# The input projection of a gated attention and convolution layer, split into a first phase of seven-product groups without attention and a second phase that holds all attention

## The chip, the cores and the metric

The kernel runs on one core of a Trainium2 chip. The metric is the device time of one execution in microseconds (us). Three runs of the kernel before took 3035.85, 3040.83 and 3042.26 us, so the median is 3040.83 us. In the text, TensorE is PE (PEld its weight loads), VectorE is DVE, ScalarE is ACT, GpSimd is POOL and SyncE, which here only issues DMAs, is SP.

## What is computed

One layer on 2048 positions of 1024 channels, all in float32. An input norm, one wide projection into nine pieces of 1024 columns, an attention branch and a convolution branch side by side, a gated merge, an output projection and a norm:

```python
h = _layer_norm(x, ln_in_g, ln_in_b)
q, k, v, z_sb, c_val, c_gate, z_cv, g_sb, g_cv = split(h @ w_in)       # 1024 -> 9 * 1024
o_sb = stick_breaking_attention(q, k, v)                               # 16 heads of 64
y_sb = (o_sb * silu(z_sb)) @ w_sb_proj
u = causal_depthwise_conv(c_val * sigmoid(c_gate), conv_w, conv_b)     # 31 taps
u = silu(_layer_norm(u, conv_ln_g, conv_ln_b))
y_cv = (u * silu(z_cv)) @ w_cv_proj
merged = sigmoid(g_sb) * y_sb + sigmoid(g_cv) * y_cv
out = _layer_norm(ALPHA * h + merged @ w_out, ln_post_g, ln_post_b)
```

The attention weight of a key is the sigmoid of its logit times the product of one minus the sigmoid over all keys between it and the query, so each row of the score matrix needs a running product along the keys.

## The kernel before

**Arithmetic.** Every float32 matrix is split exactly into two float32r parts, `a = hi + lo` (`split`, lines 112 to 114: ACT rounds into `hi` with L113, DVE subtracts into `lo` with L114). A product of two such matrices is three passes: hi times hi, hi times lo and lo times hi. A block of the projection is 128 columns of a weight by a chunk of 512 positions: 8 contraction blocks by 3 passes, 24 PE instructions of 128x512 (L194), in four "pieces" of six.

**Stages.** Positions are reversed in time and kept as four chunks of 512, in two halves: half 1 (chunks 3 and 2) is done first, then half 0 (chunks 1 and 0). The input norm writes the transposed activations of a half into `xh` and `xl`. `Fill` is the stream of projection pieces: for each half all 72 blocks of `w_in` (`fill_qkv` for k, q, v; `z`; `u`, which is c_val and c_gate; `c`, `g` and `h` for the other gates), then the two branch projections, and at the end the output projection. Weights are loaded and split again for each half (`load_w`, L148 issues the load, lines 113 and 114 split).

**Attention.** For each of 8 pairs of heads and each half of the queries: the logits of 128 queries (two PE passes, L572 and L573), ACT's sigmoid into `nb` (L575), a scan on DVE that makes the running product (L578, up to 1024 keys each), PE transposes of it (`tp`, L601), a split of the transposed tile (`th` on ACT, `tl` on DVE, L113 and L114), and the product with v (`pv`, L617). A "turn" is one transposed tile of 512 columns with its split and its product. Queries of half 0 read all keys, those of half 1 half of them, so about three quarters of the attention belong to half 0.

**What sets the order.** PE runs in the order in which the program is written. Two streams are woven by hand: the list of attention items and the `Fill` pieces, by a proportion (`spans`). Attention of half 1 lies beside the projection of half 1, as soon as a pair's q, k and v are there; attention of half 0 lies beside the projection of half 0 and the two branch projections of half 1. The other engines follow a scheduler's order, in which some evacuations are raised by `tc.high_priority`. The convolution is 31 taps on DVE (L402, one instruction of 128x512 for a tap on half the positions), issued one step at a time beside projection pieces, `PACE` = 0.83 steps for each piece (`slow_step`). All plain DMAs are issued by SP in one order (`dma`, L94; `load_w`, L148).

The two lines on which a product's cost rests:

```python
for n, (l, r) in enumerate(((wh, xh), (wh, xl), (wl, xh))):
    nc.tensor.matmul(box["ps"], lhsT=l[:, kb], rhs=r[kb], start=(kb == 0 and n == 0), stop=(kb == KB - 1 and n == 2))
```

## Time and profile before

| | |
|---|---|
| median of three runs | 3040.83 us |
| span of the profiled execution | 3036.5 us |
| DMA, mean over the span | 150 GB/s |
| ACT, share of the span | 42% |
| POOL, share of the span | 3% |

The profiled execution's span is 4.3 us below the median of the runs. The profile shows one execution. Its rows of groups read: line, engine, operation, output tile `<-` inputs, shape and count, then busy time in us and mean duration of one in ns, then the idle time of the engine before them with what ended it. Durations of consecutive instructions of one engine overlap, so the spacing of starts, not the duration, is an instruction's cost when its engine is never idle. Rows of windows give, for a stretch from A to B us, each engine's busy time with the number of instructions, the granted clock of PE as a share, the DMA engines' busy share and the rate of DMA in GB/s. The granted clock is 0.996 in the mean over the span.

### The profile page before, as it was taken

What the parts mean: (1) busy time and instruction counts of PE and PEld (TensorE: products, weight loads), DVE (VectorE), ACT (ScalarE), POOL (GpSimd) and SP (SyncE); (2) the same over time, 40 slices, a digit from 0 to 9 for tenths busy, and PEclk for the clock granted to TensorE, in tenths of its full rate; (3) what the DMA queues carried; (4) which work ended last, traced back from release to release, by engine and by line L of the source; (5) the groups of instructions that cost most, each with busy time, mean ns of one, the idle gap of its engine ahead of it and who ended that gap; (6) DMA issues with size and microseconds to landing.
All of it is one profiled execution on the core that took longest, in us unless ns stands there. A gap on an engine that the chain in (4) does not pass through costs nothing.

```text
span 3036.5 us, 41850 instructions
## 1 busy us (share of the span) xinstructions
PE 2959.8 (97%) x15304; PEld 2484.1 (82%) x15304; DVE 2381.6 (78%) x3175; ACT 1269.5 (42%) x2308; POOL 88.3 (3%) x178
## 2 busy tenths in 40 slices
PE   7999999999999999999999999999999999999998
PEld 6888888888887788888888888887888878878886
DVE  5587787777879888788879888879887788856656
ACT  5333333333336344444445444445445455533222
POOL 1000000000000000000000000000000000000000
PEclk9999999999999999999999999999999999999999
DMA  7543443434434533343335344335545666685552
GB/s 269 172 144 112 148 139 117 149 125 130 139 101 140 169 100 110 114 131 123 111 112 189 103 143 141 99 103 175 164 155 161 191 224 191 208 280 197 161 189 78
DMA packets 260221, 455.92 MB, mean 150 GB/s; under 512 B 30384, under 2 KB 55088, under 8 KB 259888
## 3 DMA queue, kind: packets, MB, share of 16 engines
q1 hardware_dynamic: 260016, 453.25, 46.0%
q8 instruction: 120, 1.97, 0.3%
q14 instruction: 85, 0.70, 0.1%
HBM read 292.70 MB, written 160.43 MB: 149 GB/s over the span
## 4 chain that ended last, share of the span: by engine, by line
PE 73%; DVE 11%; issue 10%; DMA 3%; ACT 2%; POOL 1%; SPq 0%; DVEq 0%; POOLq 0%; ACTq 0%
PE mm L194 52%; PE pv L617 7%; PE tp L601 6%; DVE nb L578 3%; PE lg L573 3%; PE lg L572 3%; DVE tl L114 2%; DVE wlo L114 1%; DVE cy L402 1%; PE mo L900 1%; DMA st<-ydq 1%; DMA ydq<-st 1%; DVE xl L114 1%; DVE st L494 0%; DVE st L493 0%
## 5 line engine op out<-in xcount | busy, mean ns | idle before, releaser
L194 PE MATMUL mm<-xh,whi 128*128 128x512 f32 x2816 | 1144.5, 406 | 1.7 <-ACT whi L113 1.5
L194 PE MATMUL mm<-xh,wlo 128*128 128x512 f32 x2816 | 1110.1, 394 | 1.4 <-DVE wlo L114 1.4
L194 PE MATMUL mm<-xl,whi 128*128 128x512 f32 x2816 | 1106.2, 393 | 1.2 <-DVE xl L114 1.2
L194 PEld LDWEIGHTS mm<-xh,wlo 128*128 128x128 f32 x2816 | 530.0, 188 | 120.9 <-DVE wlo L114 1.9
L194 PEld LDWEIGHTS mm<-xl,whi 128*128 128x128 f32 x2816 | 532.9, 189 | 86.8 <-DVE xl L114 2.4
L194 PEld LDWEIGHTS mm<-xh,whi 128*128 128x128 f32 x2816 | 531.5, 189 | 86.4 <-ACT whi L113 1.9
L113 ACT ACTIVATE th<-tp 128x512 fp32r<-128x512 f32 (+1 forms) x576 | 329.4, 572 | 613.9 <-PE tp L601 606.1
L114 DVE TENSOR_TENSOR tl<-tp,th 128x512 fp32r<-128x512 f32 (+1 forms) x576 | 376.5, 654 | 180.1 <-ACT th L113 178.2
L575 ACT ACTIVATE nb<-lg 128x512 f32<-128x512 f32 (+3 forms) x640 | 334.9, 532 | 308.9 <-PE lg L573 299.0
L578 DVE TENSOR_TENSOR_SCAN nb<-nb,dd 128x256 f32<-128x256 f32 (+7 forms) x256 | 345.1, 1350 | 42.2 <-ACT nb L575 41.5
L601 PE MATMUL tp<-ident,nb 128*128 128x128 f32 x2176 | 337.8, 274 | 20.3 <-DVE nb L578 18.2
L578 DVE TENSOR_TENSOR_SCAN nb<-nb,zero 128x1024 f32<-128x1024 f32 x128 | 300.0, 2346 | 36.5 <-ACT nb L575 36.2
L601 PEld LDWEIGHTS tp<-ident,nb 128*128 128x128 f32 x2176 | 263.4, 140 | 77.9 <-DVE nb L578 22.5
L113 ACT ACTIVATE whi<-wraw 128x512 fp32r<-128x512 f32 x352 | 217.6, 629 | 261.1 <-PE mm L194 238.8
L617 PE MATMUL pv<-tl,v 128*128 128x256 f32 (+1 forms) x1152 | 292.1, 282 | 12.2 <-DVE tl L114 11.6
L114 DVE TENSOR_TENSOR wlo<-wraw,whi 128x512 fp32r<-128x512 f32 x352 | 237.4, 682 | 80.0 <-ACT whi L113 52.9
L617 PE MATMUL pv<-th,v 128*128 128x256 f32 (+1 forms) x1152 | 299.5, 281 | 0.0
L572 PE MATMUL lg<-k,qd 128*128 128x512 f32 (+3 forms) x640 | 246.4, 386 | 11.6 <-ACT nb L575 7.0
L617 PEld LDWEIGHTS pv<-tl,v 128*128 128x128 f32 x1152 | 218.1, 189 | 36.4 <-DVE tl L114 17.2
L573 PE MATMUL lg<-k,ql 128*128 128x512 f32 (+3 forms) x640 | 233.7, 366 | 0.0
L617 PEld LDWEIGHTS pv<-th,v 128*128 128x128 f32 x1152 | 217.8, 189 | 18.5 <-issue 0.2
L402 DVE SCALAR_TENSOR_TENSOR cy<-cu,csum,cy 128x512 f32<-128x512 f32 x240 | 178.1, 742 | 4.4 <-ACT cy L398 0.9
(107 smaller groups left out, 2460.0 us busy)
## 6 DMA issues: line engine op xcount, KB each, us to landing
wraw<-in_w_in SPq DMA_DIRECT2D x288, 256.0 KB, 3.2
k<-kdr SPq DMA_DIRECT2D x192, 128.0 KB, 2.9
v<-vdr SPq DMA_DIRECT2D x96, 256.0 KB, 3.5
kdr<-st SPq DMA_DIRECT2D x64, 256.0 KB, 2.1
qdr<-st SPq DMA_DIRECT2D x64, 256.0 KB, 2.2
qd<-qdr SPq DMA_DIRECT2D x128, 128.0 KB, 2.8
vdr<-st SPq DMA_DIRECT2D x64, 256.0 KB, 2.0
xr<-in_x SPq DMA_DIRECT2D x32, 256.0 KB, 3.8
```

The source lines that it names most:

```text
L113: nc.scalar.activation(hi, src, AF.Copy)
L114: nc.vector.tensor_tensor(out=lo, in0=src, in1=hi.bitcast(F32), op=ALU.subtract)
L194: nc.tensor.matmul(box["ps"], lhsT=l[:, kb], rhs=r[kb], start=(kb == 0 and n == 0), stop=(kb == KB - 1 and n == 2))
L402: nc.vector.scalar_tensor_tensor(out=dst, in0=src[:, j:j + HN], scalar=t, in1=first, op0=ALU.mult, op1=ALU.add)
L572: nc.tensor.matmul(lg[:, :w], lhsT=qd[c][:, js], rhs=k2[kc][:, ko:ko + w], start=True, stop=False)
L573: nc.tensor.matmul(lg[:, :w], lhsT=ql[c][:, js], rhs=k2[kc][:, ko:ko + w], start=False, stop=True)
L575: nc.scalar.activation(nb[:, o:o + w], lg[:, :w], AF.Sigmoid, scale=-QS)
L578: nc.vector.tensor_tensor_scan(out=nb[:, :w], data0=nb[:, :w], data1=dd[:, :w] if diag else zero.to_broadcast([P, w]), initial=0.0 if diag ...
L601: nc.tensor.transpose(out=tp[:, at_:at_ + P], in_=tiles[j][:, so:so + P], identity=ident)
L617: nc.tensor.matmul(o[:, :w], lhsT=lv, rhs=tt[:, o0:o0 + w], start=(diag and t == 0 and n == 0 and e == 0), stop=(last and t == nt - 1 and ...
L900: nc.tensor.matmul(ps, lhsT=a[kb][:, js], rhs=b[:, kb, qs], start=(kb == 0 and n == 0), stop=(kb == KB - 1 and n == 2))
```

## The change

The main part is now in two phases.

**First phase (`first_phase`), without attention.** It computes the blocks of half 1 for all nine pieces, and of half 0 for c_val, c_gate, z_cv, g_sb and g_cv. A group takes two blocks of columns and the two chunks of a half, that is an output of 2 x 2 blocks from operands in 2 x 2 quarters. Sums and differences of quarters of the activations (`S1` to `S4`) and of the weights (`t1` to `t4`) replace one of the eight products of quarters; the seven products are accumulated in three PSUM banks (`a`, `b`, `p`), with copies from bank to bank or to SBUF in between. A product of quarters is 4 contraction blocks by 3 passes, 12 PE instructions. There are 36 groups for half 1 and 20 for half 0.

The weights of a group in half 1 are prepared on the spot: four raw quarters are loaded, DVE makes four differences, ACT makes `hi` and minus `hi`, and the low part is made by a DMA that GpSimd issues and that adds the source onto minus `hi` in SBUF. For the 20 groups that come again in half 0 all seven operands are written to DRAM and read back there; of the other 16 groups three operands are written, for use in the second phase. The activations, their sums, the gated values `u` and the running sum of the convolution go through DRAM as well. The convolution runs at one step for each piece here, and at 0.6 after it.

**Second phase.** The blocks of half 0 for q, k, v and z, in 24 instructions each as before, then the attention branch and the convolution branch projections of half 1; beside them all attention, of half 1 first (27% of the pieces), then of half 0. What follows is as before.

```diff
-PACE = 0.83
+PACES = [1.0, 0.6]
+SPLIT = 0.27
-RD = 15
+RD = 9
 def load_w(src, col):
+            if (id(src), col, g) in wdr:
+                for t, e in ((hi, 0), (lo, 1)):
+                    dma(t[:, ks], wdr[id(src), col, g][:, e])
+                continue
             raw = wp.tile([P, 4, P], F32, name="wraw", bufs=2)
...
+        XOP = ("A11", "A12", "S1", "S2", "S4", "S3", "A22")
+        P1, P2, P5, P6, P3, P7, P4 = range(7)
+        def sums(f11, f12, f21, f22, use):
+            s1, s2 = st(), st()
+            add(s1, f21, f22, ALU.add)
+            use("S1", s1)
+            add(s2, s1, f11, ALU.subtract)
+            use("S2", s2)
+            add(f12, f12, s2, ALU.subtract)
+            use("S4", f12)
+            add(f11, f11, f21, ALU.subtract)
+            use("S3", f11)
...
+        def raws(g):
+            if "kept" in g:
+                return
+            r = g["r"] = {}
+            for q, (b, k) in {"11": (0, 0), "21": (0, 1), "12": (1, 0), "22": (1, 1)}.items():
+                r[q] = raw_tile()
+                nc.sync.dma_start(out=r[q], in_=w_in[g["cols"][b] // P][:, k * 4:k * 4 + 4])
+        def w_op(g, p):
+            t = op_tile()
+            g.setdefault("w", {})[p] = t
+            if "kept" in g:
+                dma(t, g["kept"][p])
+                return
+            r = g["r"]
...
+            if p == P5:
+                r["t1"] = diff("12", "11")
+            elif p == P6:
+                r["t2"] = diff("22", "t1")
+            elif p == P7:
+                r["t3"] = diff("22", "12")
+            elif p == P4:
+                r["t4"] = diff("21", "t2")
+            src = r[{P1: "11", P2: "21", P5: "t1", P6: "t2", P3: "22", P7: "t3", P4: "t4"}[p]]
+            nc.scalar.activation(t[:, 0], src, AF.Copy)
+            low(t, src)
+            if g["keep"] and (g["keep"] == "all" or p in (P1, P2, P3)):
+                d = dram([P, 2, 4, P], F32R, f"wdr{g['cols'][0]}_{p}")
+                dma(d, t)
...
+        def low(t, src):
+            nc.scalar.activation(t[:, 1], t[:, 0].bitcast(F32), AF.Copy, scale=-1.0)
+            nc.gpsimd.dma_start(out=t[:, 1], in_=src.bitcast(F32R), accum_op=ALU.add)
+        def prod(g, p, part, bank, start=False):
+            xs_, wt = xo[XOP[p]], g["w"][p]
+            for kb in (2 * part, 2 * part + 1):
+                for n, (e, a) in enumerate(((0, 0), (0, 1), (1, 0))):
+                    nc.tensor.matmul(bank, lhsT=wt[:, e, kb], rhs=xs_[kb][a], start=start and kb == 0 and n == 0,
+                                     stop=kb == 3 and n == 2, skip_group_check=True)
...
+            def p6(part):
+                prod(g, P6, part, box["b"])
+                if part:
+                    box["u2"] = st()
+                    soon(lambda: nc.scalar.activation(box["u2"], box["b"], AF.Copy))
+            def p3(part):
+                prod(g, P3, part, box["p"])
+                if part:
+                    soon(lambda: (add(box["u2"], box["p"], box["u2"], ALU.add), use2(c1, box["u2"])))
...
+        for i in range(NPAIR):
+            fill_qkv(F, 0, i)
+            if i < NPAIR - 2:
+                F.block(*gate_z(i))
...
+        run(F, branch("s", 1), loads("c", 1))
+        run(F, branch("c", 1), loads("s", 0))
+        end = len(F.pieces) - END
+        mid = int(end * SPLIT)
+        for h, lo, hi in ((1, 0, mid), (0, mid, end)):
+            spans += [(lo + (hi - lo) * i // NPAIR, lo + (hi - lo) * (i + 1) // NPAIR) for i in range(NPAIR)]
```

How the order of the engines moves is shown at three places. The first is PE beside the attention. Before, in the half-0 part of the main phase, PE has six projection instructions (`mm`, of which `xh`, `xl` are activations and `whi`, `wlo` weights) between two pieces of attention (`lg` logits, `pv` the product with v, `th` and `tl` the split tile):

```order
L194 MATMUL mm_12700<-xh_8954,whi_12571 128x512
L194 MATMUL mm_12700<-xl_8955,whi_12571 128x512
L194 MATMUL mm_12700<-xh_8954,wlo_12572 128x512
L194 MATMUL mm_12700<-xh_8980,whi_12571 128x512
L194 MATMUL mm_12700<-xl_8981,whi_12571 128x512
L194 MATMUL mm_12700<-xh_8980,wlo_12572 128x512
L572 MATMUL lg_12707<-k2_12077,qd_12058 128x512
L573 MATMUL lg_12707<-k2_12077,ql00_569 128x512
L617 MATMUL pv_12712<-th_12657,v2_12070 128x256
L617 MATMUL pv_12712<-tl_12658,v2_12070 128x256
```

In the second phase of the change PE has, in the half-0 part too, several pieces of attention behind each other (`tp` the transposes of `nb`; the activations are now named by quarter, `A22h`, `A22l`):

```order
L201 MATMUL mm<-A22h,w_15234 128x512
L201 MATMUL mm<-A22l,w_15234 128x512
L201 MATMUL mm<-A22h,w_15235 128x512
L583 MATMUL lg<-k_15614,qd 128x384
L584 MATMUL lg<-k_15614,ql_10879 128x384
L628 MATMUL pv<-th,v_15617 128x256
L628 MATMUL pv<-tl,v_15617 128x256
L628 MATMUL pv<-th,v_15617 128x128
L628 MATMUL pv<-tl,v_15617 128x128
L612 MATMUL tp<-ident,nb 128x128 x4
L628 MATMUL pv<-th,v_15627 128x256
L628 MATMUL pv<-tl,v_15627 128x256
```

Projection work moved out from between the attention pieces: 2304 projection instructions are left beside the 576 turns.

The second place is SP's queue in the first phase. Before, in the part of half 1, SP has loads of raw weights (`wraw`) between the stores and loads of k, q, v and of the gates (`kdr`, `k_`, `gat`):

```order
L94 DMA gat_4b<-st 128x512
L148 DMA wraw<-in_w_in 128x512
L94 DMA kdr_5_266<-st 128x512 x2
L94 DMA k_6646<-kdr_5_266 64x512 x2
L94 DMA kdr_5_258<-st 128x512
L148 DMA wraw<-in_w_in 128x512
```

In the first phase of the change, also half 1, stores of prepared weights stand between them (`wdr`, 128x1024, that is 512 KB each; `fdr` and `sdrS` are activations and their sums for half 0):

```order
L867 DMA wrx<-in_w_in 128x512
L93 DMA gat_0s<-st 128x512
L93 DMA wdr_0_2860<-w_2856 128x1024
L93 DMA st<-fdr_497 128x512 x2
L93 DMA st<-fdr_496 128x512 x2
L93 DMA wdr_1_2866<-w_2862 128x1024
L93 DMA wdr_2_2892<-w_2886 128x1024
L93 DMA gat_0c<-st 128x512
L93 DMA sdrS_0_500<-st 128x512
L93 DMA sdrS_0_504<-st 128x512
```

The loads and stores of attention are gone from this stretch, and stores of weights and of sums have come in; the 252 accumulating DMAs stand in GpSimd's queue beside them.

The third place is DVE beside the attention of half 0. Before (`nb` a scan, `tl` the low part of a turn, `wlo` the low part of a weight, `cu` the gated value of the convolution):

```order
L114 TENSOR_TENSOR tl_18270<-tp_18264,th_18269 128x512
L114 TENSOR_TENSOR tl_18295<-tp_18289,th_18294 128x512
L114 TENSOR_TENSOR wlo_18348<-wraw_18349,whi_18347 128x512
L114 TENSOR_TENSOR wlo_18348<-wraw_18353,whi_18347 128x512
L114 TENSOR_TENSOR tl_18316<-tp_18310,th_18315 128x512
L578 SCALAR_TENSOR_TENSOR nb_18326<-nb_18326,nb_18210,zero_577 128x1024
L578 SCALAR_TENSOR_TENSOR nb_18342<-nb_18342,nb_18247,zero_577 128x1024
L375 TENSOR_TENSOR cu_18378<-mm_18319,gt_18243 128x256x2
```

In the second phase of the change (`og` is the attention's output, `st` with `mu` and `st` with `st` are the norm over the channels of the convolution):

```order
L589 SCALAR_TENSOR_TENSOR nb_17901<-nb_17901,nb_17799,zero_10886 128x1024
L504 TENSOR_TENSOR st_17890<-st_17890,st_17891 128x512
L589 SCALAR_TENSOR_TENSOR nb_17911<-nb_17911,nb_17825,zero_10886 128x1024
L117 TENSOR_TENSOR tl_17936<-tp_17931,th_17935 128x384
L642 TENSOR_TENSOR og_17957<-pv_17533,st_17958 64x512
L117 TENSOR_TENSOR tl_17967<-tp_17961,th_17966 128x512
L505 TENSOR_TENSOR st_17892<-st_17890,st_17892 128x512
L589 SCALAR_TENSOR_TENSOR nb_17947<-nb_17947,dd_10875 128x512
L589 SCALAR_TENSOR_TENSOR nb_17977<-nb_17977,dd_10875 128x384
L501 TENSOR_TENSOR st_17997<-st_17997,mu_16940 128x512
```

Between the first and the last scan on DVE stand, by the order of the change, all 384 scans, 571 low parts of turns, 129 convolution taps, 32 low parts of v (256 columns) and some 450 other instructions of 512 columns, among them the norm of the convolution for three chunks; 13 of the 16 convolution blocks come ahead of the first scan.

More of the change, by code (lines that the diff above doesn't have):

```diff
@@ L141, in load_w @@
     def load_w(src, col):
[L143 to L144 removed]
+        hi, lo = (wp.tile([P, KB, P], F32R, name="w4", bufs=4) for _ in range(2))
         for g in range(2):
             ks = slice(g * 4, g * 4 + 4)
+            if (id(src), col, g) in wdr:
+                for t, e in ((hi, 0), (lo, 1)):
+                    dma(t[:, ks], wdr[id(src), col, g][:, e])
+                continue
             raw = wp.tile([P, 4, P], F32, name="wraw", bufs=2)
@@ new lines, in normed @@
+    def normed(c, j, xr):
+        rb = c * 4 + j
+        bs = sm.tile([P, 2, 6], F32, name="bs")
+        for q in range(2):
+            nc.sync.dma_start(out=xr[q], in_=x[rb * P:(rb + 1) * P, q * CH:(q + 1) * CH])
+            nc.vector.bn_stats(out=bs[:, q], in_=xr[q])
+        nc.vector.bn_aggr(out=mrs[:, rb], in_=bs)
+        rsqrt_eps(mrs[:, rb, 1:2], mrs[:, rb, 1:2], 1)
+        nm = negmean(mrs[:, rb])
+        nc.vector.tensor_scalar(out=xr[0], in0=xr[0], scalar1=mrs[:, rb, 0:1], scalar2=mrs[:, rb, 1:2],
+                                op0=ALU.subtract, op1=ALU.mult)
+        nc.scalar.activation(xr[1], xr[1], AF.Identity, scale=mrs[:, rb, 1:2], bias=nm)
+        return xr
@@ L385, in layer_kernel, with load_u, load_next @@
     ysum = {}
     convs = []
-    def conv(m, h, u):
+    us = {}
+    def load_u(m, h):
+        u = us[m, h] = cv_p.tile([P, 2, HN + H0], F32, name="cu", bufs=2)
+        dma(u[:, :, :HN], udr[h, m])
+        if h == 1:
+            nc.gpsimd.memset(u[:, :, HN:HN + H1], 0.0)
+        else:
+            dma(u[:, :, HN:HN + H1], udr[1, m][:, :, :H1])
+    def load_next():
+        if len(slow) > 1:
+            nxt = keys[slow[1]]
+            if nxt not in us:
+                load_u(*nxt)
+    keys = {}
@@ L721, in loads, with fill_qkv @@
         return [load_acts((n, c), srcs[n], c) for c in half(h)]
-    def fill_qkv(F, h, i, first=None):
-        one = (w_in, COL_K + i * P, xs(h), use_qk(kdr, i))
-        two = (w_in, COL_Q + i * P, xs(h), use_qk(qdr, i))
-        if first is not None:
-            F.pair(one, two, first)
-        else:
-            F.block(*one)
-            F.block(*two)
-        block_v(F, i, h)
-        F.delay(9 if h or i else RD, 0, lambda: ready.__setitem__((h, i), True))
+    def fill_qkv(F, h, i):
+        F.block(w_in, COL_K + i * P, xs(h), use_qk(kdr, i))
+        F.block(w_in, COL_Q + i * P, xs(h), use_qk(qdr, i))
+        block_v(F, i, h)
+        F.delay(RD, 0, lambda: ready.__setitem__((h, i), True))
@@ L734, in layer_kernel, with c1_of @@
+    def c1_of(g):
+        return half(g["h"])[0]
     ready = {}
@@ L740, in layer_kernel @@
     pace = [0]
+    phase = [0]
     def newest():
@@ L747, in slow_step @@
         marks.append(newest())
-        pace[0] += PACE
+        pace[0] += PACES[phase[0]]
         if not now and (not slow or pace[0] < 1):
@@ L763, in emit_fill @@
                 slow_step()
+    with ExitStack() as s1:
+        x2 = s1.enter_context(tc.tile_pool(name="x2", bufs=4))
+        w1 = s1.enter_context(tc.tile_pool(name="w1", bufs=6))
+        ps_p = s1.enter_context(tc.tile_pool(name="psp", bufs=2, space=PS))
+        first_phase(F, x2, w1, ps_p)
+        assert not F.later
+        emit_fill(len(F.pieces))
+    F = Fill()
+    n_done[0] = 0
+    phase[0] = 1
     with ExitStack() as s2:
@@ new lines, in gate_z @@
+        def gate_z(m):
+            return w_in, COL_Z + m * P, xs(0), silu_to(m, "b")
+        for i in range(NPAIR):
+            ready[1, i] = True
+        norm = conv_mean(1) + conv_ln(3) + conv_ln(2)
+        for i in range(NPAIR):
+            fill_qkv(F, 0, i)
+            if i < NPAIR - 2:
+                F.block(*gate_z(i))
+            for q in range(10):
+                if norm and i >= I0:
+                    F.delay(1 + 3 * q, 0.1, norm.pop(0))
+        F.pair(gate_z(NPAIR - 2), gate_z(NPAIR - 1), freed=loads("s", 1))
```

447 lines of the change are left out of this document (304 added, 143 removed).

## Prediction

> **What bounds the kernel now.** I read the page first: the span, the busy times and the chain that ended last.
>
> ```profile
> span 3036.5 us, 41850 instructions
> ...
> PE 2959.8 (97%) x15304; PEld 2484.1 (82%) x15304; DVE 2381.6 (78%) x3175; ACT 1269.5 (42%) x2308; POOL 88.3 (3%) x178
> ...
> PE 73%; DVE 11%; issue 10%; DMA 3%; ACT 2%; POOL 1%; SPq 0%; DVEq 0%; POOLq 0%; ACTq 0%
> ```
>
> PE is busy nearly all the time and leads the chain, and DVE comes second. A busy PE is not a PE at its peak, so the next view is the chain in order of time, cut to a few pieces at 2410 us. The columns are start, length and what.
>
> ```profile
> 2410.17 1.39 PE mm L194 x6
> 2411.56 0.44 PE tp L601 x4
> 2412.17 0.53 PE pv L617 x4
> ...
> 2415.92 0.23 PE lg L572
> 2416.16 0.23 PE lg L573
> 2416.39 0.47 PE pv L617 x4
> ```
>
> Six projection matmuls follow each other in 1.39 us, so one costs 0.232 us, although its duration is shown as about 0.4 us. Four transposes cost 0.44, four products with v 0.47, a pair of logits of 512 columns 0.46. The counts are in the page's groups:
>
> ```profile
> L194 PE MATMUL mm<-xh,whi 128*128 128x512 f32 x2816 | 1144.5, 406 | 1.7 <-ACT whi L113 1.5
> ...
> L601 PE MATMUL tp<-ident,nb 128*128 128x128 f32 x2176 | 337.8, 274 | 20.3 <-DVE nb L578 18.2
> ...
> L617 PE MATMUL pv<-tl,v 128*128 128x256 f32 (+1 forms) x1152 | 292.1, 282 | 12.2 <-DVE tl L114 11.6
> ...
> L572 PE MATMUL lg<-k,qd 128*128 128x512 f32 (+3 forms) x640 | 246.4, 386 | 11.6 <-ACT nb L575 7.0
> ```
>
> The first row is one of three alike, so 8448 projection matmuls: 1957 us. Attention is 2176 transposes (239 us), 2304 products (271 us, some 256 of them half as wide, so 256) and 640 pairs of logits (294 us if all were 512 wide; 192 are narrower, so about 253): 748 us. The output projection adds 768 matmuls at 0.229 (436 starts in 100 us, window below), 176 us, and the transposes of input and v and the small products some 38. Together 2919 of 3036.5 us: before, PE works at **96%** of what its own spacing allows.
>
> **The windows** show how much room its neighbours have.
>
> ```profile
> 0.00:100.00 100.00, 83.70 (x393) 67.57 (x394) 54.91 (x100) 50.40 (x87) 14.28 (x36) 1.00 0.80 269
> ...
> 1600.00:1700.00 100.00, 97.35 (x522) 82.11 (x521) 96.31 (x127) 50.63 (x93) 1.48 (x3) 1.00 0.56 181
> ...
> 2400.00:2500.00 100.00, 93.32 (x524) 79.34 (x522) 82.80 (x105) 52.20 (x95) 1.02 (x1) 1.00 0.66 212
> ...
> 2800.00:2900.00 100.00, 100.00 (x436) 81.65 (x435) 67.10 (x105) 28.06 (x39) 5.63 (x15) 1.00 0.54 176
> ```
>
> After the engines (PE, PEld, DVE, ACT, POOL) come PE's clock, the DMA engines' share and GB/s. DVE can be 96% busy for 100 us with little loss on PE. No window of 100 us has more than 269 GB/s.
>
> **The change, part by part.**
>
> *PE's work.* By the order, the first phase has 56 groups of 84 matmuls, 4704 (3024 for half 1, 1680 for half 0), and 32 blocks of 48 stay, 1536. That is 6240 where 6912 stood: 672 fewer at 0.232 us, **156 us** less for PE. If nothing else mattered and PE kept its 96%, the time would be 2763 / 0.96 = 2880 us. What follows asks which stage can take it.
>
> *The tail.* Behind the last attention nothing changes:
>
> ```profile
> 2655.00:3037.00 382.00, 368.79 (x1613) 300.55 (x1611) 233.92 (x354) 112.07 (x155) 16.95 (x47) 0.99 0.54 180
> ```
>
> Term: 380 us.
>
> *First phase, half 1: PE.* 36 groups are 3024 x 0.232 = 701 us. The first 100 us have 270 projection matmuls before:
>
> ```profile
> 0.00:100.00 100.00, 69.27 (x270) 51.13 (x271) 1.00 0.80 269
> ```
>
> They take 63 us, and the other 123 of the 393 instructions some 0.11 us each, 14, so the start costs about 23 us. In the change the sums S1 to S4 need some nine DVE instructions of 0.6 us for each of four blocks ahead of the third product, and the weights of the second group are asked for only behind the third product, which I put at another 21. So **745 us at PE's pace**.
>
> *First phase, half 1: DMA.* By SP's order up to the last raw weight load, 207 MB: 93 of prepared weights written, 38 of raw weights, 76 of the rest. GpSimd's 252 accumulating DMAs bring 66 MB. 273 MB in 745 us are 367 GB/s, against 150 in the mean before. How much can the DMA engines move? The page's totals, and four windows of 5 us in which their share is about 1:
>
> ```profile
> DMA packets 260221, 455.92 MB, mean 150 GB/s; under 512 B 30384, under 2 KB 55088, under 8 KB 259888
> ...
> 10.00:15.00 5.00, 1.00 0.96 345
> 80.00:85.00 5.00, 1.00 1.04 401
> 2670.00:2675.00 5.00, 1.00 0.97 344
> 2695.00:2700.00 5.00, 1.00 1.01 369
> ...
> wraw<-in_w_in SPq DMA_DIRECT2D x288, 256.0 KB, 3.2
> ```
>
> The last row is a load of raw weights on SP: 3.2 us from issue to landing. I take 345 GB/s as what is held, 401 as the best. An accumulating DMA isn't in the trace. Bounds: as one copy of 256 KB, or as two, since it moves a second operand. As one, 273 MB / 345 = 793 us; as two, 340 MB / 345 = 984 us; at 401 and one copy 682, so PE's 745 would end last. A copy reads and writes each byte once; an accumulate has two operands to read and one result to write, three moves for two, so I take 1.5 copies: 307 MB / 345 = **890 us**, DMA-bound. This is the largest unknown, 745 to 984.
>
> The Trainium skill (Collectives: The Full Stack, "The bandwidth ceiling: the fold count and why AG ≠ RS ≠ AR") says that a reducing transfer needs two source reads on the same ring, and so delivers half of what a copy does. By it the accumulates count as two copies, which is the third rival below; no run here shows one yet.
>
> *DVE and ACT there* have room: DVE's work ahead of the first scan (some 500 instructions of 512 columns by 0.6 us, 607 convolution taps by 0.66, and small ones) is near 780 us in 1290. What hides the copies between banks is the product in between (12 x 0.232 = 2.8 us); each group has four such turns, and where an evacuation is queued behind an instruction that waits for a late raw weight, PE waits too. In a DMA-bound stretch this is inside the 890; elsewhere I put it at nothing, at most half an instruction (0.3 us) in each of 224 turns, 67 us.
>
> *First phase, half 0.* 1680 x 0.232 = 390 us. 115 MB of DMA in it are 295 GB/s, above any window of 100 us but below 345. Nine buffers for operands give some eight products of lead. Term: 400.
>
> *Second phase: PE.* 2304 projection matmuls, 534 us, attention 748, transposes of v 7: 1290 us.
>
> *Second phase: DVE.* Between the first and the last scan the order has nearly all attention, the last convolution blocks, the splits of half 0 and three quarters of the norm over the channels. Durations:
>
> ```profile
> L114 DVE TENSOR_TENSOR tl<-tp,th 128x512 fp32r<-128x512 f32 (+1 forms) x576 | 376.5, 654 | 180.1 <-ACT th L113 178.2
> ...
> L578 DVE TENSOR_TENSOR_SCAN nb<-nb,dd 128x256 f32<-128x256 f32 (+7 forms) x256 | 345.1, 1350 | 42.2 <-ACT nb L575 41.5
> ...
> L578 DVE TENSOR_TENSOR_SCAN nb<-nb,zero 128x1024 f32<-128x1024 f32 x128 | 300.0, 2346 | 36.5 <-ACT nb L575 36.2
> ...
> L114 DVE TENSOR_TENSOR wlo<-wraw,whi 128x512 fp32r<-128x512 f32 x352 | 237.4, 682 | 80.0 <-ACT whi L113 52.9
> ...
> L402 DVE SCALAR_TENSOR_TENSOR cy<-cu,csum,cy 128x512 f32<-128x512 f32 x240 | 178.1, 742 | 4.4 <-ACT cy L398 0.9
> ...
> L114 DVE TENSOR_TENSOR st<-tp,st 128x256 fp32r<-128x256 f32 x64 | 26.7, 417 | 17.5 <-ACT st L113 17.3
> ```
>
> Scans 645 us, 571 turns by 0.654, 373, 450 others of 512 columns by 0.682, 307, 129 taps by 0.742, 96, 32 of 256 columns by 0.417, 13: 1434 us. In a queue that never empties the starts are closer than the durations:
>
> ```profile
> 1639.30 2.34 DVE L578 TENSOR_TENSOR_SCAN nb<-nb,zero 128x1024 f32<-128x1024 f32 x1
> 1641.56 0.66 DVE L114 TENSOR_TENSOR tl<-tp,th 128x512 fp32r<-128x512 f32 x1
> 1642.15 0.70 DVE L494 TENSOR_TENSOR st<-st 128x512 f32<-128x512 f32 x1
> ```
>
> The scan gives way 0.08 us before its end, so about 1566 instructions save 125 us: DVE needs at least **1310 us** where PE needs 1290. Before, DVE had a fifth of its time free while it fed the attention; here neither has any. The turns come every 2.5 us, not every 4, so a transposed tile has less time to be split before its product is due, and it can stand behind a scan of 2.3 us. From below: PE alone at 96%, 1345 us. From above: DVE by full durations at the 94% that lies between the windows' 83 and 96, 1434 / 0.94 = 1525. I take 1310 / 0.90 = **1450 us**, nearest to what the busy windows bear.
>
> *Sum against the profiled execution:* 890 + 400 + 1450 + 380 = **3120 us**, 2.7% above the span of 3036.5. The median of the runs is 4 us above that span, which the rounding covers.
>
> **The rivals.**
>
> *DMA keeps up, DVE does not.* Accumulates cost one copy and the engines hold 367 GB/s. For it: 401 was reached for 5 us. Against it: 269 over 100 us. 745 + 400 + 1450 + 380 = 2975: **faster**. It decides where half 1 of the first phase takes less than 806 us.
>
> *Both keep up.* DVE reaches the 96% of its best window throughout: 745 + 390 + 1345 + 380 = 2860. Against it: at 2400 to 2500 us PE loses time with DVE at 83%.
>
> *Accumulates cost two copies,* and SP's stores of weights, which wait for them, hold up raw loads behind them in its queue: 984 + 410 + 1450 + 380 = 3224: slower by 6%.
>
> *The gain is hidden:* the losses of the second phase just eat the 156 us and the first phase holds 800 us, near 3036.
>
> **How the numbers follow.** Forecast, DMA-bound half 1 and a strained DVE (3045 to 3180 us): 0.42. DMA keeps up: 0.23. Both keep up: 0.09. Two copies or worse: 0.21. Hidden, within 0.2% or 6 us of before, which is about what a measurement of this kernel can tell from no change: 0.05. So faster 0.32, same 0.05, slower 0.63. The range leaves out about a tenth on each side, so it cuts into the second rival below (2930) and reaches past the third above (3270).
>
> **What would show it.** Right: in half 1 of the first phase a DMA share near 1 at 300 GB/s or more, PE idle behind GpSimd's accumulates or raw weights, groups 24 us apart instead of 19.5; later DVE above 90% with PE waiting for `nb` and `tl`, about 2.5 us for each turn. Wrong: PE spaced by 0.232 us through the first phase; accumulating DMAs that land as fast as the 3.2 us of a raw weight; or a first phase that waits for copies between banks with the DMA share far below 1, where the step "room on ACT and DVE" fails.

## The result, and the profile after

The changed kernel takes 3353.05 us (median of 4 runs, 3351.98 to 3357.53) where the kernel before, on the same chip, takes 3040.59: a ratio of **1.1036**, 95% interval 1.102 to 1.1052. It is slower, as forecast, by four times as much (312 us for 79), and lies above the range (3045 to 3180 us). One run of the kernel e12 below took 3604.51 us at a granted clock of 0.75, where its other three took 3060 to 3076 us at 0.98 to 0.99, and no time below includes it.

The page of the changed kernel, the lines that answer to those of before: span, busy times, the 40 slices (PE, DMA share, granted clock; one slice is 84 us), the DMA queues (packets, MB, time as a share of 16 engines' span) and the chain.

```profile
span 3351.0 us, 42860 instructions
...
PE 2948.6 (88%) x14666; PEld 2433.7 (73%) x14666; DVE 2423.2 (72%) x3219; ACT 1540.5 (46%) x2792; POOL 291.8 (9%) x414
...
PE   6676788878888999989998998999899989889998
...
PEclk9888888989899999999999999999999999989999
DMA  7999999999999877675656344354543544478462
...
q1 hardware_dynamic: 327696, 640.05, 57.3%
q0 software_dynamic: 36288, 66.08, 11.4%
...
PE 36%; DVE 17%; issue 11%; DMA 6%; ACT 3%; SPq 1%; POOL 1%; DVEq 0%; POOLq 0%; ACTq 0%
```

PE led the chain with 73% before and has 36% now. The slices show two losses of different kinds: for the first twelve the DMA engines are full and PE is not; from slice 17 on the DMA engines are half idle and PE still does not fill. The stages, from the starts of their matmuls: first product at 26 us, half 1 of the first phase until 1033, half 0 until 1423, attention from 1434 to 2949, tail to 3351. The windows of these stages (PE, PEld, DVE, ACT, POOL, then PE's clock, DMA share, GB/s):

```profile
26.00:1033.00 1007.00, 799.75 (x3232) 633.49 (x3231) 556.15 (x852) 508.72 (x906) 238.63 (x306) 0.89 0.98 280
1034.00:1423.00 389.00, 387.20 (x1678) 314.54 (x1677) 248.30 (x346) 86.91 (x144) 1.97 (x4) 1.00 0.78 258
1434.00:2949.00 1515.00, 1382.58 (x8155) 1179.66 (x8156) 1339.58 (x1580) 799.14 (x1541) 19.34 (x27) 0.98 0.50 158
```

| stage | predicted | measured | off by |
|---|---|---|---|
| first phase, half 1 | 890 | 1033 | +143 |
| first phase, half 0 | 400 | 390 | -10 |
| second phase | 1450 | 1526 | +76 |
| tail | 380 | 402 | +22 |
| sum | 3120 | 3351 | +231 |

In half 1 the DMA engines are busy 98% of 1007 us, at 280 GB/s and no more, and PE waits. They are busy from the start: in the 26 us ahead of the first product their share is 0.93 at 284 GB/s. In half 0 the groups follow each other at PE's own pace: 387 us busy of 389. In the second phase DVE is busy 88% of the time, PE 91%, and neither leads.

What PE waits for in half 1, and DVE behind it (engine, tile and line, what ended the wait; us in total, times, longest):

```profile
PE pb L910 <- DVE gt L757: 85.3, 24, 8.9
```

```profile
DVE wrx L757 <- DMA wrx<-in_w_in: 119.5, 27, 12.7
```

PE's bank `pb` waits for a sum on DVE, and DVE, at the same line, waits for raw weights: what stands in DVE's queue behind a late load is late with it. SP's queue waits as well, in the same stretch; its longest row is:

```profile
SPq L93 <- DMA w4x<-wrx: 130.9, 47, 24.2
```

With its three sister rows (`w<-wrx`, `w4x<-wraw`, `w<-wraw`: 95, 66 and 62 us) SP waits 354 us for accumulates to land, and the raw loads behind its stores wait with it, as the prediction's third rival put it. Since the DMA engines are busy 98% of the time all the same, these waits can have cost little beyond the engines' own time. The landing times of DMAs (KB each, median us from issue) show the load too:

```profile
wdr<-w4x SPq DMA_DIRECT2D x108, 512.0 KB, 5.4
...
w4x<-wrx POOLq DMA_DIRECT2D x100, 256.0 KB, 6.2
...
wrx<-in_w_in SPq DMA_DIRECT2D x72, 256.0 KB, 5.5
```

A raw load (`wraw` before, here `wrx`, all in half 1) took 3.2 us before and takes 5.5; an accumulate of the same size takes 6.2. The groups of attention, to set beside those of before (idle time of PE before them: 20.3 and 12.2 us then):

```profile
L612 PE MATMUL tp<-ident,nb 128*128 128x128 f32 x2176 | 352.7, 278 | 74.1 <-DVE nb L589 58.5
...
L628 PE MATMUL pv<-tl,v 128*128 128x256 f32 (+1 forms) x1152 | 303.2, 292 | 43.4 <-DVE tl L117 42.5
```

### The profile page after: what moved, and what is told of

It reads as the page before. It is cut to its first block, busy times and chain, and to the rows that moved or that the text cites. A ratio compares the mean times of both kernels' runs of the same rounds, so it can differ in the third digit from the quotient of the medians.

```text
span 3351.0 us, 42860 instructions
## 1 busy us (share of the span) xinstructions
PE 2948.6 (88%) x14666; PEld 2433.7 (73%) x14666; DVE 2423.2 (72%) x3219; ACT 1540.5 (46%) x2792; POOL 291.8 (9%) x414
## 3 DMA queue, kind: packets, MB, share of 16 engines
q1 hardware_dynamic: 327696, 640.05, 57.3%
q0 software_dynamic: 36288, 66.08, 11.4%
## 4 chain that ended last, share of the span: by engine, by line
PE 36%; DVE 17%; issue 11%; DMA 6%; ACT 3%; SPq 1%; POOL 1%; DVEq 0%; POOLq 0%; ACTq 0%
PE mm L201 10%; DVE nb L589 8%; PE pb L910 6%; PE pp L910 4%; PE mm L910 4%; PE pv L628 4%; DVE tl L117 4%; PE tp L612 4%; PE lg L583 2%; PE lg L584 2%; SPq L93 1%; ACT nb L586 1%; ACT th L116 1%; DMA st<-ydq 1%; PE mo L1242 1%
## 5 line engine op out<-in xcount | busy, mean ns | idle before, releaser
L612 PE MATMUL tp<-ident,nb 128*128 128x128 f32 x2176 | 352.7, 278 | 74.1 <-DVE nb L589 58.5
L589 DVE TENSOR_TENSOR_SCAN nb<-nb,zero 128x1024 f32<-128x1024 f32 x128 | 299.8, 2345 | 22.3 <-ACT nb L586 22.0
L583 PE MATMUL lg<-k,qd 128*128 128x512 f32 (+3 forms) x640 | 267.6, 419 | 22.3 <-ACT nb L586 10.7
L201 PE MATMUL mm<-A11h,w 128*128 128x512 f32 x512 | 184.4, 406 | 11.6 <-ACT w L116 6.1
L201 PE MATMUL mm<-SXh,w 128*128 128x512 f32 x512 | 183.9, 405 | 1.9 <-DVE st L712 1.9
L201 PE MATMUL mm<-A12h,w 128*128 128x512 f32 x512 | 184.4, 406 | 0.0
L201 PE MATMUL mm<-A22h,w 128*128 128x512 f32 x512 | 183.5, 405 | 0.0
L409 DVE SCALAR_TENSOR_TENSOR cu<-cd,cwt,cu 128x512 f32<-128x512 f32 x240 | 178.8, 745 | 4.2
L409 DVE SCALAR_TENSOR_TENSOR cy<-cu,cwt,cy 128x512 f32<-128x512 f32 x240 | 178.7, 745 | 3.4
L583 PEld LDWEIGHTS lg<-k,qd 128*128 128x128 f32 x640 | 122.0, 191 | 47.1 <-ACT nb L586 28.4
L910 PE MATMUL pb<-A22h,w4x 128*128 128x512 f32 x256 | 99.7, 454 | 49.0 <-DVE gt L757 49.0
```

The costliest lines, as they stand in the source:

```text
L409: nc.vector.scalar_tensor_tensor(out=dst, in0=src[:, j:j + HN], scalar=t, in1=first, op0=ALU.mult, op1=ALU.add)
L583: nc.tensor.matmul(lg[:, :w], lhsT=qd[c][:, js], rhs=k2[kc][:, ko:ko + w], start=True, stop=False)
L589: nc.vector.tensor_tensor_scan(out=nb[:, :w], data0=nb[:, :w], data1=dd[:, :w] if diag else zero.to_broadcast([P, w]), initial=0.0 if diag ...
L612: nc.tensor.transpose(out=tp[:, at_:at_ + P], in_=tiles[j][:, so:so + P], identity=ident)
L910: nc.tensor.matmul(bank, lhsT=wt[:, e, kb], rhs=xs_[kb][a], start=start and kb == 0 and n == 0, stop=kb == 3 and n == 2, skip_group_check= ...
```

## The experiments

Two questions are open in this profile. What fills the DMA engines in half 1: the accumulates, the stores of weights, or something that only looks like DMA? And what holds the second phase, where no engine is full? Each kernel below had one run beside a run of the kernel before, unless an interval is given; the median of the kernel before was 3040 to 3044 us beside them. Executions of one kernel differ by 0.3 to 0.5% here, so a difference of 15 us between two single runs is not clear of that.

**First question: the DMA engines.** e1: the low parts by one subtraction on DVE, as before the change, in place of ACT's minus `hi` and the accumulate.

```diff
-nc.scalar.activation(t[:, 1], t[:, 0].bitcast(F32), AF.Copy, scale=-1.0)
-nc.gpsimd.dma_start(out=t[:, 1], in_=src.bitcast(F32R), accum_op=ALU.add)
+nc.vector.tensor_tensor(out=t[:, 1], in0=src, in1=t[:, 0].bitcast(F32), op=ALU.subtract)
```

> Low parts of the first phase's weights by one DVE subtraction each instead of a negative copy on ACT and an accumulating DMA on GpSimd's queue; nothing else changed. Theory A (the DMA engines are full in half 1 of the first phase, and an accumulate costs two copies): the demand falls from 207 + 2 x 66 = 339 MB to 207 MB, 615 us at the 338 GB/s that this makes of the changed kernel's 1003 us, so PE's pace ends last: half 1 ends at 760 to 800 us instead of 1033, the later stages stay at 390, 1530 and 398, total about 3090 to 3120. Rival B (copies between banks and DVE's queue hold PE, not the bytes): DVE gets 252 more instructions, 150 us, half 1 still ends after 950, total above 3270.

Measured: 3134.03 us, half 1 until 811: theory A's way, 14 and 11 us above its ranges, and far from rival B. Its page has no queue q0 any more, and this q1; below it the window of its half 1:

```profile
q1 hardware_dynamic: 327696, 640.05, 61.6%
```

```profile
26.00:811.00 785.00, 743.13 (x3220) 599.47 (x3219) 664.42 (x1059) 357.80 (x651) 34.47 (x61) 0.98 0.78 274
```

222 us of the stage went with the 66 MB of accumulates, while the bytes of all other DMAs stayed the same and their time too: 61.6% of 3132 us is 1929 us, 57.3% of 3351 is 1920. So an accumulate's price can be read off the page after: q0 took 11.4% of 3351 us, 382 us of all engines, for 66.08 MB, that is 173 GB/s, where q1 moved 640 MB at 333 GB/s. **An accumulate costs 1.9 copies**, or 2.0 against the 345 GB/s of the prediction. Why it costs that (a second read, or something else) no run here separates.

e2: the accumulates stay, but the operands that come again in half 0 are prepared again there instead of being stored and read back.

```diff
-if h == 0:
-    g["kept"] = kept[e, m]
-else:
-    g["keep"] = "some" if e in "kqvz" else "all"
-    g["to"] = kept.setdefault((e, m), {})
+g["keep"] = "some" if e in "kqvz" else ""
```

> The 20 groups that come twice prepare their weights again in half 0, instead of writing them in half 1 and reading them back; the accumulates stay. Theory A (bytes): half 1 loses 73 MB of writes, 134 + 2 x 66 = 266 MB, 787 us at 338 GB/s, so it ends near 815 instead of 1033; half 0 needs 136 MB with its accumulates doubled, about 405 to 430 us instead of 390; total 3140 to 3180. Rival C (the latency of the accumulates in their queue, not the bytes of all, sets the pace): half 1 still ends after 980, and half 0, which gets 140 accumulates, slows to 500 or more; total above 3400.

Measured: 3259.39 us, half 1 until 919, half 0 in 410. The DMA share in its half 1 is still high:

```profile
100.00:800.00 700.00, 608.12 (x2540) 484.09 (x2540) 436.42 (x668) 391.98 (x701) 197.06 (x250) 0.94 0.93 245
```

The total lies between theory A and rival C. Half 1 lost 114 us, half of what the bytes promised. 245 GB/s fill the engines to 93% here, since more of what is left is accumulates, and its page prices them a second time:

```profile
q1 hardware_dynamic: 298896, 514.20, 48.2%
q0 software_dynamic: 56448, 102.79, 18.6%
```

102.79 MB in 18.6% of 3258 us are 170 GB/s, beside 327 for q1, again 1.9 copies. What kept the other half of the promise away is that the engines are no longer full: over the whole stage, 26 to 919 us, their share is 0.90 at 234 GB/s, and DVE waits 144 us there for accumulates to land before it can write a buffer again (`wrx` behind `w<-wrx` 94 us, behind `w4x<-wrx` 50). So a part of rival C holds too; no run took it apart. e3 has both edits.

> Both edits: no accumulating DMA and no kept weights. Theory A: with DMA out of the way twice over, half 1 is no faster than with the first edit alone, 760 to 800 us, since PE's 84 x 0.232 us for each group end last; half 0 gets 220 more DVE instructions, 130 us on about 260, so 390 to 420 us; total 3090 to 3140. Rival B: what is left above 745 us in half 1 is copies between banks, up to 67 us in both halves.

Measured: 3108.71 us, half 1 until 794, half 0 in 389. The windows of its three stages:

```profile
26.00:794.00 768.00, 733.76 (x3221) 592.06 (x3221) 692.92 (x1105) 361.33 (x661) 30.57 (x60) 0.99 0.55 185
794.00:1183.00 389.00, 388.04 (x1682) 315.31 (x1681) 369.48 (x567) 162.16 (x278) 1.97 (x4) 1.00 0.40 127
1194.00:2708.00 1514.00, 1381.67 (x8154) 1179.21 (x8155) 1340.03 (x1580) 799.19 (x1541) 19.31 (x27) 0.98 0.50 158
```

With the DMA engines 45% idle half 1 is only 17 us faster than in e1. So 794 is what the stage takes without a DMA bound: by the starts of every 84th product its first group takes 42 us, the next eleven 22.4 on average (the input's transposes stand between the products there) and the other 24 take 20.0, where half 0's take 19.5. The second phase is the same to 1 us as in the change, whatever came before it.

e4 asks what the two phases cost alone. It is e3 with plain blocks of 24 in place of the groups in the first phase; the weights for the second phase are still kept.

```diff
-groups = [group(1, *o) for o in order(1)] + [group(0, *o) for o in order(0)]
...
+for h in (1, 0):
+    todo = [b for o in order(h) for b in blks(h, *o)]
+    for b, after in todo[:-2]:
+        F.block(*b, after=after)
```

> Two phases as in the change, but the first phase in plain products (24 instructions for each block and chunk, 5376 instead of 4704), low parts by DVE, no kept weights but those for the second phase, no sums. It isolates the two phases. If the second phase is slow for its own density (DVE), it stays at 1500 to 1560 us, the first takes 5376 x 0.232 = 1247 and a start of 25 to 45, 1270 to 1300, the tail 398: total 3190 to 3240, so that the two phases alone cost 150 to 200 us against the kernel before. If the second phase is slow because of what the first leaves behind, it falls below 1450 and the total below 3130.

Measured: 3183.86 us, 140 us more than before the change with the same arithmetic, 6 below the range of the theory that the second phase is slow for its own density.

```profile
37.00:1264.00 1227.00, 1224.69 (x5460) 1012.97 (x5459) 776.24 (x1136) 295.32 (x552) 32.05 (x59) 1.00 0.46 150
1274.00:2782.00 1508.00, 1378.86 (x8159) 1177.23 (x8158) 1315.83 (x1540) 798.03 (x1543) 18.05 (x27) 0.99 0.49 155
```

The first phase is full to 2 us in 1227; nearly all of the 140 is lost behind it, in the second phase and the tail. Against this kernel the groups of seven gain 75 us (e3) of the 156 that PE's count gives: the first phase ends at 1183 for 1264. Where PE runs nothing else, the plain blocks' matmuls start 0.2275 us apart on average here (800 to 1260 us), those of the groups in e3's half 0 0.231, which takes some 20 of the 156 (5376 by 0.2275 less 4704 by 0.231 are 136); the slow first groups of half 1 take most of the rest (768 us for 3024 by 0.231, 699).

**Second question: the second phase.** All of these but e8 start from e3. e5 takes DVE's work on the turns away: the low part of the transposed tile is left out, and the products with v read the high part twice.

```diff
-    split(tp[:, :at_], th[:, :at_], tl[:, :at_])
-box["t"] = th, tl
+    nc.scalar.activation(th[:, :at_], tp[:, :at_], AF.Copy)
+box["t"] = th, th
```

> On the kernel with both edits of the first phase (3109 us, second phase 1183 to 2708). The low part of each turn is left out: the products with v read the high part twice, so PE does the same work and DVE loses 576 instructions, 343 us, in the second phase alone. Theory A (DVE's time bounds the second phase): its demand falls from 1310 to 967 us, PE's 1290 at 96% ends last, the second phase takes 1345 to 1390 instead of 1525, total 2930 to 2975. Rival D (PE and the two other engines hold each other in the chain logits, scan, transposes, whatever DVE's load): it stays above 1460, total above 3045.

Measured: 3033.77 us. It lies between theory A and rival D, nearer to D. 373 us of durations left DVE, its busy time in the stretch of attention fell by 320 (1340 to 1020), and the stretch by 79, from 1514 to 1436.

e6 moves 188 sums and products of 512 columns from DVE to GpSimd (one of six lines):

```diff
-nc.vector.tensor_tensor(out=y, in0=y, in1=s, op=ALU.mult)
+nc.gpsimd.tensor_tensor(out=y, in0=y, in1=s, op=ALU.mult)
```

> On the same kernel: 192 element-wise instructions on SBUF (the sum of squares and two products of the channel norm, two steps of the attention's output, one sum of the branch) go from DVE to GpSimd, some 150 of them, 90 us, in the second phase. Theory A: the second phase falls by 60 to 90 us, total 3020 to 3050. Rival D: it stays within 25 us, total 3085 to 3135; it rises if GpSimd's instructions are slow and the attention's output waits for them.

Measured: 3166.13 us, 57 us slower than e3. One of the groups on GpSimd, and DVE's long scan, in e6 (busy us, mean ns):

```profile
L505 POOL TENSOR_TENSOR st<-st 128x512 f32<-128x512 f32 x32 | 65.7, 2052 | 2.5
...
L589 DVE TENSOR_TENSOR_SCAN nb<-nb,zero 128x1024 f32<-128x1024 f32 x128 | 310.8, 2431 | 29.1 <-ACT nb L586 28.7
```

The scan took 2345 ns on the page after and takes 2431 here; the moved instructions take 1.4 to 2.1 us each where DVE needed about 0.7 (676 to 698 ns in e3). In the stretch of attention 145 of them took 99 us of durations off DVE, but the 1435 that stayed grew from 1336 to 1401, and the stretch from 1514 to 1557. The splits `tl`, which read one input from PSUM, did not grow (681 and 680 ns). The theory missed its sign. How much of the 57 us comes from the slower DVE and how much from waits for GpSimd was not separated.

e8 does the same on top of e1, with the convolution run faster in the first phase, so that less of it is left for the second (the order of the blocks changes with it).

```diff
-PACES = [1.0, 0.6]
+PACES = [1.6, 0.6]
```

> Low parts by DVE (3134 us), weights kept, the same work on GpSimd, and the convolution taken faster in the first phase (1.6 steps for each piece, its blocks early in half 0), so that one of 16 blocks instead of three is left for the second. DVE loses 90 + 62 us there. Theory A: the second phase falls by 110 to 150 us, half 0, where DVE is idle a third of the time, rises by less than 15; total 2990 to 3040, about as fast as the kernel before. Rival D: total above 3090.

Measured: 3179.06 us, 45 above e1. The two edits were not run apart; GpSimd's part cost 57 us in e6, so by that the earlier convolution gained some 12.

e7 takes PE's work away: the projections of the second phase leave out the pass with the low parts of the weights, 768 matmuls.

```diff
-for n, (l, r) in enumerate(((wh, xh), (wh, xl), (wl, xh))):
+for n, (l, r) in enumerate(((wh, xh), (wh, xl), (wl, xh))[:2 if phase[0] == 1 else 3]):
```

> On the same kernel: the projection products of the second phase leave out the pass of the low weights, so PE loses 768 instructions, 178 us, there, DVE loses nothing. Theory A: the second phase is held by DVE and stays within 45 us of 1525, total 3065 to 3110. Rival E (PE's own work bounds it, with a fixed loss to waits): it falls by 130 to 178 us, total 2930 to 2980.

Measured: 3030.69 us. 178 us less for PE are 76 us less in the stretch of attention (1438), between the two theories.

e10 makes the scans earlier: more buffers for their results, and more lead.

```diff
-NBW = 4
-LEAD = 4.0
+NBW = 6
+LEAD = 8.0
...
-k2[c] = kv.tile([P, CH], F32R, name="k2", bufs=8)
+k2[c] = kv.tile([P, CH], F32R, name="k2", bufs=6)
...
-v2[c] = kv.tile([P, 4, P], F32R, name="v2", bufs=8)
+v2[c] = kv.tile([P, 4, P], F32R, name="v2", bufs=6)
```

> e3 with the scans of the attention made further ahead: six buffers for their results instead of four, a lead of eight turns of work instead of four, and for room six buffers each for keys and values instead of eight. Nothing is left out. Theory A (PE and DVE are coupled because transposes find the scan just behind time; a scan that is made earlier takes the waits of tp for nb, 43 us in 1300, and part of those of pv for tl): the second phase falls by 40 to 100 us and the total is 3010 to 3070. Rival B (the waits go back to DVE's order, split behind scan, whatever the lead): within 25 us of e3, 3085 to 3135. Rival C (keys and values with two buffers fewer are loaded too late): above 3135, with waits of lg for k or v.

Measured: 3149.79 us, 41 slower than e3. That is rival C's time without its sign: PE waits once for keys, 10.5 us, as it does in e3 (10.4). e11 makes the products with v later instead, and has seven buffers for keys and values where e3 has eight.

```diff
-th = at.tile([P, CH], F32R, name="th", bufs=2)
-tl = at.tile([P, CH], F32R, name="tl", bufs=2)
+th = at.tile([P, CH], F32R, name="th", bufs=3)
+tl = at.tile([P, CH], F32R, name="tl", bufs=3)
...
-if len(queue) == 2:
+if len(queue) == 3:
```

> e3 with the product with v of each turn put three turns behind its transposes instead of two, three buffers instead of two for the halves of the transposed tile, and seven buffers each for keys and values instead of eight. Nothing is left out. Theory A (a split has too little time before its product is due, because it stands behind a scan on DVE): the waits of pv for tl, 42 us in 1300 in e3, fall below 15, the second phase falls by 30 to 70, total 3040 to 3075. Rival B (as in e10, what is taken from one wait comes back in another, because DVE's share of 89% with instructions of 2.3 us in it is itself the limit): pv for tl falls, tp for nb or for tl rises by as much, total 3085 to 3130.

Measured: 3094.04 us, 15 less than e3, which two single runs cannot tell from no change, and inside rival B's range. PE's waits from 1300 to 2600 us in e3, in e10 and in e11:

```profile
PE tp L612 <- DVE nb L589: 45.5, 45, 4.0
PE pv L628 <- DVE tl L117: 42.2, 64, 4.0
PE tp L612 <- DVE tl L117: 13.1, 13, 1.7
```

```profile
PE pv L628 <- DVE tl L117: 92.9, 93, 3.7
PE lg L583 <- ACT nb L586: 20.7, 54, 2.3
PE tp L612 <- DVE tl L117: 9.4, 11, 3.1
```

```profile
PE tp L612 <- DVE nb L589: 58.4, 47, 3.7
PE tp L612 <- DVE tl L117: 33.9, 44, 2.2
```

With more lead the waits for scans are gone, and those for splits have doubled: the scans went ahead of the splits in the same queue. With more time for the splits, the products no longer wait for them; the transposes wait more, for the scans and for a `tp` bank that is not split yet. The waits of these three rows were 101 us in e3, and 92 in e11: a wait taken away in one place of DVE's queue comes back in another.

e13 has the cuts of e5 and e7 together.

> e3 with both cuts of e5 and e7: the low part of each transposed turn is left out (the products with v read the high part twice) and the projections of the second phase leave out the pass with the low parts of the weights. Theory A (in the second phase both engines are close to full and each waits for the other; each cut alone is worth 75 us, since the other engine then holds the pace): both together give at least the sum, the second phase falls from 1514 to 1280 to 1340, total 2880 to 2940. Rival B (one chain of logits, sigmoid, scan, transposes, split and product of fixed length holds each turn to some 2.5 us, whatever the engines' load): both together give little more than one, at most 100 us: total 3005 to 3035.

Measured: 2908.87 us, and 1312 us for the stretch of attention, inside theory A's numbers. The cuts alone gave 79 and 76; together they give 202. The windows of e5, e7 and e13 in that stretch:

```profile
1300.00:2500.00 1200.00, 1133.58 (x6843) 982.91 (x6842) 854.22 (x834) 665.00 (x1293) 15.06 (x23) 0.99 0.52 166
```

```profile
1300.00:2500.00 1200.00, 1037.19 (x6201) 876.34 (x6199) 1115.58 (x1317) 669.99 (x1294) 16.67 (x23) 0.98 0.52 165
```

```profile
1300.00:2400.00 1100.00, 1002.25 (x6275) 872.15 (x6273) 858.86 (x845) 669.24 (x1304) 17.67 (x24) 0.99 0.57 181
```

Relieve DVE, and PE is 94% busy; relieve PE, and DVE is 93% busy; relieve both, and the phase moves. A chain of fixed length for each turn would have stopped e13 near 1430. But full engines are not the whole of it. PE's work in e13 is 1107 us, counted as in the table below, so 205 us are still lost, where e3 loses 231, although DVE is busy for only 77% of the stretch (1014 of 1312 us). What PE waits for most in e13, from 1300 to 2400 us, is still a scan:

```profile
PE tp L612 <- DVE nb L589: 79.6, 68, 3.2
```

No run gave e13's kernel more buffers or more lead, so why the scans are late beside a DVE with room stays open.

**Thinner attention.** e9 (on e1) makes only half 1 in groups of seven; all of half 0 is left, in plain blocks, as filling between the turns. The convolution runs at 0.83 steps for each piece in the second phase, as before the change. Its core:

```diff
-groups = [group(1, *o) for o in order(1)] + [group(0, *o) for o in order(0)]
+groups = [group(1, *o) for o in order(1)]
...
-            if i < NPAIR - 2:
-                F.block(*gate_z(i))
+            F.block(*gate_z(i))
+            gated_blocks(i)
+            left = rest_of(i)
+            for b in left[:1] if i == NPAIR - 1 else left:
+                F.block(*b)
```

> Low parts of the weights by one DVE subtraction (as in e1), and only half 1 of the first phase is made in groups of seven products (36 groups, 3024 matmuls); all of half 0 is made in plain blocks of 48 beside the attention (72 blocks, 3456 matmuls instead of 2304 in the second phase). Nothing is left out. Theory A (the attention's turns couple PE and DVE only where they come every 2.6 us; with half as much again of projection between them, some 3.6 us for each turn, PE fills the waits as it did before the change at 96%): half 1 ends at about 800 us as in e3, then (2919 - 701 - 23 - 368 = about 1735 us of PE work) / 0.96 = 1807, and 398 for the tail: 3000, 2960 to 3040. Rival B (the loss belongs to the attention's chain itself, however thin it is spread; PE stays at the 85% of the second phase): 800 + 2040 + 398 = 3240. Rival C (the weights kept for half 0 of all kinds cost DMA time again): half 1 ends at 900 or later, and the rest follows A or B: 3100 or more.

Measured: 3079.56 us, ratio to before 1.0124, 95% interval 1.0106 to 1.0142; between A and B, and without C's sign (half 1 ends at 787). e12 adds the edit of e11.

> e9 with the change of e11: products with v three turns behind, three buffers for the halves, seven for keys and values. Nothing is left out. Theory A as in e11, in thinner attention: waits of pv for tl, 12 us in 1200 in e9, and part of the 24 us of tp for nb go: total 3035 to 3060, about the time before the change. Rival B: no change within 15 us of e9's 3080: 3065 to 3095.

Measured: 3064.56 us (median of three runs, 3060.42 to 3076.3), ratio 1.0095, 95% interval 1.0066 to 1.0125; between the two theories. It is the best of the versions with nothing left out, though its interval overlaps that of e9, and still about 1% slower than the kernel before.

Three kernels that leave nothing out, side by side: the stretch from the first to the last matmul of attention, and an estimate of PE's work in it (the projections counted in the trace by 0.232 us, plus 755 us of attention and small transposes; 778 before, with the small products that lie in its stretch). The rows of the stretches of the kernel before and of e9 (that of e3 stands above):

```profile
73.00:2660.00 2587.00, 2538.30 (x13464) 2141.90 (x13463) 2112.91 (x2747) 1120.53 (x2093) 57.10 (x95) 1.00 0.44 142
799.00:2683.00 1884.00, 1796.62 (x10077) 1532.14 (x10077) 1560.81 (x1891) 861.01 (x1632) 20.09 (x27) 0.99 0.50 159
```

| kernel | stretch, us | us for each of 576 turns | projections in it | PE's work | share | DVE busy |
|---|---|---|---|---|---|---|
| before | 2587 | 4.49 | 7447 | 2506 | 97% | 82% |
| e9 | 1884 | 3.27 | 4195 | 1728 | 92% | 83% |
| e3 (the change takes 1515) | 1514 | 2.63 | 2275 | 1283 | 85% | 89% |

The closer the turns, the less of its work PE gets done in the time: 81 us lost, then 156, then 231. DVE's share alone does not explain this: it is nearly the same in e9 as before, where PE's loss has already doubled. Nor does the distance of the turns alone: in e5, with turns 2.49 us apart and less work on DVE, PE loses 153 us (1436 less 1283).

## Why the prediction was wrong

**The accumulates.** The step that failed most is "three moves for two, so I take 1.5 copies: 307 MB / 345 = 890 us". The runs show 2.0 copies at that rate, 382 us where 1.5 copies of 66 MB are 287. With two copies the working gave 984 of the 1033. The bytes make up the rest: 280 GB/s over 1007 us and 284 over the first 26 are 289 MB, 16 more than the 273 summed, which take 47 us at 345 GB/s. The rate held (333 for 345). The Trainium skill (Collectives: The Full Stack, "The bandwidth ceiling: the fold count and why AG ≠ RS ≠ AR") gives the reducing transfer of a collective two source reads and half the rate; the trace agrees for this local one, 173 GB/s beside 333. The prediction had both bounds, no row for the operation, and took the middle; the mechanism was the third rival's, whose total of 3224 missed by the second phase (76 us), in half 1 (49, nearly all for its bytes) and in the tail (22).

**PE's pace in half 1.** "745 us at PE's pace" was too low: e3 takes 794 with the DMA engines 45% idle. The start costs what the prediction gave it (27 us ahead of the first product for 23, and 22 more in the first group for 21); what it put at nothing is the eleven groups behind it, 32 us above half 0's 19.5 each, and 12 us over the rest of the stage. So the rivals that ended faster were not open, even without accumulates: 794 + 389 + 1525 + 399 is e3's time.

**Half 0 and the turnarounds.** Right: 390 us for 400, and 389 of them are 1680 matmuls at 0.232. The copies between banks cost nothing, as put, out of a DMA-bound stretch; e3's half 0 groups take 19.5 us, 84 by 0.232.

**The second phase.** "I take 1310 / 0.90" failed: DVE had 1340 us of work there, 30 more than summed, and was busy for 88% of it. The places named were right (PE waits for `nb` and `tl`, 101 us of its idle time after), the view was not: the prediction divided one engine's work by a share taken from stretches where the other engine had room or was the bound. e5, e7 and e13 show that both hold it: PE's 1283 us and DVE's 1340 us lie in the same 1515, the two wait for each other at many turns, and less work on one side is worth about a quarter (320 us of DVE's busy time for 79) or less than half (PE's 178 for 76) of its size. That both are nearly full is not the whole reason, by e13 and by the table. e4 shows that the dense second phase, and no full DMA engine (share 0.49) and little of the clock (0.99, at most 15 of 1508 us), is the price of the two phases: 140 us with plain arithmetic.

**The tail** took 402 us for 380, and 399 in e3: some 20 us of waits of PE in its first 100 us for sums and weights of the two branches. It was not tested what brings them.

What stays open is what a dense turn loses in detail: e10 and e11 moved the waits and changed the sum little, and PE's waits that the profile names are 140 of the 231 us that it loses in e3's stretch. The clock there, 0.98, is at most 30 us of it (0.02 of 1514).

## What to carry to other kernels

An operation that the trace does not show is priced by a bound, and the forecast belongs at the bound to which its mechanism points (here two operands to read, and two copies measured), not in the middle. Two engines that hand each tile to each other and each need nearly the whole time need not reach the larger of the two: here 1283 and 1340 us of work took 1515, and moving unrelated work out from between the turns took away what had filled the gaps. An eighth of a stage's PE instructions saved is worth nearly its size where PE is alone on the path, as in half 0, and not where it waits for others, as at the start of half 1.

## What the runs showed of the hardware

- An accumulating DMA from SBUF to SBUF moved 173 GB/s over 16 engines' time, copies in the same run 333 (after); 170 and 327 in e2.
- In the DMA-bound stretch PE's granted clock fell to 0.89 (PE busy 79%); it was 0.94 in e2 (87%, 100 to 800 us) and 0.99 in e3 (96%). A matmul takes longer for it: behind a wait of 6.4 us, the clock of 87.6 to 94.2 us is 0.50, and the starts of 128x512 matmuls are some 0.43 us apart there, 0.23 after it. The prediction went by 0.232 us throughout. The Trainium skill (TensorE: Matmul & The Clock Gate, "Part 1: The HAM clock gate (the "warmup" mystery)") has the gate fall to half after an idle window of some 3.4 us; the trace fits that (the wait of 6.4 us and the 0.50 behind it). No cost of it shows in the DMA-bound stretch, where the DMA engines were busy 98%.
- Elementwise work of 512 columns took 1.4 to 2.1 us on GpSimd (e6), and DVE's scans of 1024 columns beside it grew from 2345 (e3) to 2431 ns, those of 128 columns from 411 to 578, while splits with one input from PSUM stayed at 680.
